# A list scheduler with other durations and a shared-access rule for VectorE and GpSimd

## The chip, the core and the metric

The kernel runs on one core of a Trainium2 chip. The metric is the device time of one execution in microseconds (us), lower is better. TensorE (PE, with its weight loads PEld), VectorE (DVE), ScalarE (ACT), GpSimd (POOL) and the DMA queue of SyncE (SP) each work through a list of instructions of their own, in order, and wait for each other by semaphores.

## What is computed

A small transformer in fp32: 512 tokens, model width 1024, three layers. Layer one has latent attention (12 heads) and cross attention to 256 memory tokens, layer two sliding-window attention (12 query heads, 4 key heads, window 128) and again the cross attention, each with a squared-ReLU MLP of width 4096. The third layer joins a convolution path with a sparse attention of three branches (8 heads) and has a gated convolutional MLP of width 2816.

```
for i in range(2):
    hn = rmsnorm(x, attn_norm_g[i])
    mix, q_cross = (mla_mixer if i == 0 else swa_mixer)(hn, ...)
    cross = memory_cross_attention(q_cross, mem_n, w_mem_kv[i])
    x = x + concat([mix, cross]) @ w_o[i]
    x = x + squared_relu_mlp(rmsnorm(x, mlp_norm_g[i]), w_up[i], w_down[i])
x = rmsnorm(x, final_norm_g)
...
y_b = nsa(q, k_cmp, v_cmp, k_sel, v_sel, k_win, v_win, gates)
mix = gm0 * (y_a @ w_a_out) + gm1 * (y_b @ w_b_out)
x = x + mix @ w_o
x = x + (silu(conv(gate)) * up) @ w_ffn_out
```

## The kernel before

Activations lie transposed, features on the 128 partitions and the 512 tokens along the free axis, so a matrix product is a row of 128x128 weight blocks against 128x512 activations. Every product in the dense layers is made of three matmuls: weights and activations are split into a high part (a cast to fp32r) and a low part (the rest), and high-high, high-low and low-high are added in PSUM. The weights come in chunks of 128x512: a DMA into one of four buffers `raw`, a cast on ScalarE into one of eight buffers `h`, a subtraction on VectorE into one of eight buffers `l` (`fetch_chunk`).

An attention head goes: score matmuls into a PSUM bank `pss`, a fused add-and-minimum on VectorE (the page shows it as CUSTOM_DVE_ANT_0 with a READ_ACCUMULATOR, the order as ISA) that writes the masked scores to SBUF, the exponential on ScalarE with its sum, a reciprocal on VectorE (`rinv`), then `normalize`: four `tensor_scalar` operations on GpSimd, one for each block of 128 queries. TensorE transposes the result into a bank `pst`; ScalarE casts it (high) and VectorE subtracts (low) into tiles `pgr`; value matmuls add into the bank `pso`; `o_out` copies one half on ScalarE and adds on VectorE; `os_set` splits the pair of heads again into high and low. `wo` is the output projection: three jobs are woven, and the k-blocks come in the order 6, 7, 0 to 5, so that the last pair of heads is needed last. Its matmuls and the next heads' projections, in the three banks `psd`, are what TensorE can do while it waits for a softmax.

None of this is issued as written. `Trace` records all 13187 operations with their tiles, `add` gives each a cost by `_op_cost` and finds the operations it depends on, and `schedule` is a greedy list scheduler: it keeps one clock per engine (`engt`), takes the earliest operation that can start, the first recorded one among the ready (a few are recorded as earlier by a bias), and gives out buffers as it goes. A result becomes visible to another engine after `AFTER` of the producer plus `BEFORE` of the consumer. The result is one order for all operations; `emit` issues each in that order, and each engine gets its part as its list. The planned times are not kept: on the chip an engine waits for operands and buffers only.

All recorded instructions carry the one line of the call in `emit` (L426 in the profile), so groups go by tile: `psd`, `pss`, `pst` and `pso` are the banks, `pgf` fp32 pages of 128x512, `pgr` their fp32r kind, `sm` small tiles, `x` the residual, `raw`, `h`, `l` the weights.

## Time and profile before

| | |
|---|---|
| median of 3 runs | 1854.27 us (1851.56 to 1854.47) |
| the profiled execution, its own time | 1850.78 us |
| its span, first to last instruction | 1849.0 us, mean granted clock 0.999 |
| TensorE busy | 1829.8 us, 99% |
| VectorE, ScalarE, GpSimd busy | 1166.8, 856.3, 168.1 us |
| waits of weight loads for the transposes on GpSimd | 9.7 us, 23 times |

The stages by the timeline: first projections to 76 us, latent and cross attention to 198 us, output projection and MLP to 620 us, the second layer's attention to 714 us, its projection and MLP to 1101 us, the third layer's projections and attention to 1320 us, its merging and gates to 1488 us, the last MLP to the end. A matmul's busy time overlaps the next one's, so a busy TensorE may still hold small gaps; those show as waits by releaser, and as idle time in brackets in a timeline.

### The profile page before, as it was taken

What the parts mean: (1) busy time and instruction counts of PE and PEld (TensorE: products, weight loads), DVE (VectorE), ACT (ScalarE), POOL (GpSimd) and SP (SyncE); (2) the same over time, 40 slices, a digit from 0 to 9 for tenths busy, and PEclk for the clock granted to TensorE, in tenths of its full rate; (3) what the DMA queues carried; (4) which work ended last, traced back from release to release, by engine and by line L of the source; (5) the groups of instructions that cost most, each with busy time, mean ns of one, the idle gap of its engine ahead of it and who ended that gap; (6) DMA issues with size and microseconds to landing.
All of it is one profiled execution on the core that took longest, in us unless ns stands there. A gap on an engine that the chain in (4) does not pass through costs nothing.

```text
span 1849.0 us, 24977 instructions
## 1 busy us (share of the span) xinstructions
PE 1829.8 (99%) x8767; PEld 1516.9 (82%) x8767; DVE 1166.8 (63%) x2383; ACT 856.3 (46%) x1700; POOL 168.1 (9%) x228
## 2 busy tenths in 40 slices
PE   8999999999999999999999999999999999999999
PEld 6877888888888888888888887888888888888887
DVE  8998954344446897545434476888655567763752
ACT  7788544242324786443423245476533344442421
POOL 0033100000000241000000000134100011110100
PEclk9999999999999999999999999999999999999999
DMA  6421233333333212333333323212133333333332
GB/s 197 128 58 47 75 97 98 97 97 97 98 97 91 63 52 75 97 97 103 97 97 97 97 67 89 74 47 80 58 97 97 97 97 95 99 93 101 97 97 76
DMA packets 92151, 167.01 MB, mean 90 GB/s; under 512 B 10612, under 2 KB 12408, under 8 KB 92024
## 3 DMA queue, kind: packets, MB, share of 16 engines
q1 hardware_dynamic: 92024, 165.40, 30.1%
q8 instruction: 69, 1.13, 0.2%
q14 instruction: 58, 0.48, 0.1%
HBM read 161.69 MB, written 2.10 MB: 89 GB/s over the span
## 4 chain that ended last, share of the span: by engine, by line
PE 92%; DVE 2%; ACT 2%; issue 1%; POOL 1%; DMA 1%; SPq 1%; POOLq 0%; DVEq 0%; ACTq 0%
PE psd L426 82%; PE pst L426 4%; PE pss L426 4%; PE pso L426 3%; DVE pgf L426 1%; POOL pgf L426 1%; DMA raw<-w 1%; ACT pgf L426 1%; SPq L426 1%; DVE pgr L426 0%; ACT pgr L426 0%; ACT h L426 0%; DVE l L426 0%; DVE sm L426 0%; ACT L426 0%
## 5 line engine op out<-in xcount | busy, mean ns | idle before, releaser
L426 PE MATMUL psd<-pgr,h 128*128 128x512 f32 (+1 forms) x4590 | 1429.8, 390 | 9.0 <-ACT pgr L426 8.5
L426 PEld LDWEIGHTS psd<-pgr,h 128*128 128x128 f32 x4590 | 856.1, 188 | 181.8 <-ACT pgr L426 8.9
L426 PE MATMUL psd<-pgr,l 128*128 128x512 f32 (+1 forms) x2295 | 894.7, 390 | 1.1 <-DVE l L426 1.1
L426 DVE TENSOR_TENSOR l<-raw,h 128x512 fp32r<-128x512 f32 (+2 forms) x601 | 434.2, 726 | 449.2 <-ACT h L426 445.7
L426 ACT CAST h<-raw 128x512 fp32r<-128x512 f32 (+2 forms) x601 | 369.0, 616 | 677.0 <-PE psd L426 605.7
L426 PEld LDWEIGHTS psd<-pgr,l 128*128 128x128 f32 x2295 | 431.0, 188 | 88.5 <-DVE l L426 1.8
L426 POOL TENSOR_SCALAR pgf<-pgf,sm 128x256 f32<-128x256 f32 (+3 forms) x128 | 76.3, 613 | 618.7 <-DVE sm L426 591.9
L426 ACT CAST pgr<-pgf 128x512 fp32r<-128x512 f32 (+4 forms) x184 | 108.2, 590 | 46.3 <-POOL pgf L426 29.9
L426 DVE TENSOR_TENSOR pgr<-pgf,pgr 128x512 fp32r<-128x512 f32 (+4 forms) x184 | 121.5, 662 | 10.7 <-ACT pgr L426 5.6
L426 ACT ACTIVATE pgf<-pgf 128x512 f32<-128x512 f32 (+2 forms) x125 | 74.7, 603 | 108.5 <-DVE pgf L426 106.8
L426 POOL TENSOR_SCALAR pgf<-pgf,sm,gates 128x128 f32<-128x128 f32 (+1 forms) x64 | 49.9, 793 | 549.5 <-PE psd L426 477.8
L426 DVE TENSOR_TENSOR pgf<-psd,pgf 128x512 f32<-128x512 f32 (+2 forms) x94 | 61.3, 654 | 46.5 <-PE psd L426 45.9
L426 PE MATMUL pso<-pgr,pgr 128*128 128x512 f32 (+3 forms) x368 | 89.4, 339 | 0.1
L426 DVE TENSOR_TENSOR pgr<-pst,pgr 128x512 fp32r<-128x512 f32 (+1 forms) x126 | 73.9, 610 | 9.0 <-ACT pgr L426 8.3
L426 POOL TENSOR_TENSOR pgf<-pgf,pgf 128x512 f32<-128x512 f32 x30 | 40.7, 1358 | 422.9 <-DVE pgf L426 412.9
L426 PE MATMUL pst<-cstt,pgf 128*128 128x128 f32 x436 | 76.1, 276 | 2.9 <-POOL pgf L426 2.7
L426 ACT CAST pgr<-pst 128x512 fp32r<-128x512 f32 (+1 forms) x126 | 62.9, 530 | 25.7 <-PE pst L426 23.7
L426 DVE CUSTOM_DVE_ANT_0 pgf<-pss,cmask 128x256 f32<-128x256 f32 (+3 forms) x144 | 65.1, 468 | 9.6 <-PE pss L426 7.9
L426 DVE TENSOR_TENSOR x<-psd,x 128x512 f32<-128x512 f32 x80 | 55.1, 690 | 25.0 <-PE psd L426 24.9
L426 ACT ACTIVATE pgf<-pgf,sm 128x256 f32<-128x256 f32 (+3 forms) x128 | 66.0, 518 | 8.1 <-DVE sm L426 7.4
L426 DVE TENSOR_TENSOR pgf<-pgf,pgf 128x512 f32<-128x512 f32 (+2 forms) x103 | 66.4, 656 | 5.2 <-DMA pgf<-pgf 4.5
L426 PEld LDWEIGHTS pso<-pgr,pgr 128*128 128x128 f32 x368 | 58.8, 189 | 13.0 <-issue 2.5
(120 smaller groups left out, 1075.3 us busy)
## 6 DMA issues: line engine op xcount, KB each, us to landing
raw<-w SPq DMA_DIRECT2D x588, 256.0 KB, 2.6
x<-xT SPq DMA_DIRECT2D x8, 256.0 KB, 5.9
out<-x SPq DMA_DIRECT2D x8, 256.0 KB, 2.0
pgf<-pgf SPq DMA_DIRECT2D x24, 64.0 KB, 2.0
pgf<-aux SPq DMA_DIRECT2D x5, 256.0 KB, 2.7
pgf<-memT SPq DMA_DIRECT2D x4, 256.0 KB, 4.6
raw<-w SPq DMA_DIRECT2D x7, 140.0 KB, 2.1
raw<-w SPq DMA_DIRECT2D x4, 192.0 KB, 2.6
```

The costliest lines, as they stand in the source:

```text
L426: getattr(getattr(nc, names[o.eng]), o.method)(*[r(x) for x in o.args], **{k: r(v) for k, v in o.kw.items()})
```

## The change

The change touches the planner alone. The recorded operations, their dependencies, the priorities, the buffers and the delays `AFTER` and `BEFORE` stay. `_op_cost` gets other durations: a 512-column fp32r matmul counts 226.7 ns where it counted 215.8, a 256-column one 120 in place of 109, a 256 KB load on SP 655 in place of 831, ScalarE 95 ns more for each operand that is one column, 110 in place of 220 for an accumulated sum, GpSimd 25 or 50 ns more. And `schedule` knows a port: an operation of GpSimd other than a memset, and an operation of VectorE of four kinds with all its tiles in SBUF, starts in the plan only when the other engine's last such operation has ended.

```diff
--- before.py
+++ after.py
@@ -303,8 +303,20 @@
 BEFORE = {"PE": 135.0, "DVE": 0.0, "ACT": 0.0, "POOL": 45.0, "SP": 0.0}
 
 
+PORT = ("DVE", "POOL")
+
+
+def _uses_port(o):
+
+    if o.eng == "POOL":
+        return o.method != "memset"
+    if o.eng != "DVE" or any(v.tile.whole for v in o.reads + o.writes):
+        return False
+    return o.method in ("tensor_tensor", "scalar_tensor_tensor", "tensor_scalar", "tensor_copy")
+
+
 class Op:
-    __slots__ = ("i", "eng", "method", "args", "kw", "reads", "writes", "cost", "preds", "succs", "tiles",
+    __slots__ = ("port", "i", "eng", "method", "args", "kw", "reads", "writes", "cost", "preds", "succs", "tiles",
                  "prio", "bias", "npred", "est", "end")
 
 
@@ -319,21 +331,26 @@
     if eng == "PE":
         if method == "transpose":
             return 109.0
-        m, k = _free(args[1]) / 1.2, _free(args[2]) * 0.4167
-        return (max(2 * m, 4 * k) if args[2].dtype == FT else max(m, k)) + 2.5
+        k = _free(args[2])
+        if args[2].dtype == FT:
+            return 2 * max(111.0, (2 * k + 8) / 2.4)
+        return max(105.0, (k + 32) / 2.4)
     if eng == "SP":
-        return 60.0 + n * writes[0].shape[0] * 4 / 340.0
+        return max(600.0, n * writes[0].shape[0] * 4 / 400.0)
+    scalars = [x for x in list(args[2:4]) + [kw.get(k) for k in ("scalar", "bias", "scale")]
+               if isinstance(x, View) and _free(x) == 1]
     if eng == "ACT":
-        return 0.833 * n + (52 if psum else 93) + (220 if accum else 0)
-    scalars = [x for x in list(args[2:4]) + [kw.get("scalar")] if isinstance(x, View) and _free(x) == 1]
+        return 0.833 * n + (52 if psum else 93) + 95 * len(scalars) + (110 if accum else 0)
     if eng == "POOL":
         if method == "memset":
             return 0.833 * n + 60
         if method == "tensor_tensor":
-            return 2.2 * n + 100
-        return 0.833 * n + 160 + 64 * len(scalars)
+            return 2.2 * n + 150
+        return 0.833 * n + 185 + 64 * len(scalars) + (340 if scalars and scalars[0].tile.name.startswith("vecs") else 0)
     n = max([n] + [_free(v) for v in reads if method == "tensor_reduce"])
-    extra = 68 + (60 if scalars or accum else 0)
+    extra = 68 + (60 if scalars else 0) + (75 if accum else 0)
+    if n == 1:
+        return 70.0
     if method in ("tensor_copy", "tensor_scalar", "memset") and not psum:
         return 0.521 * n + extra
     return 1.042 * n + extra
@@ -414,6 +431,7 @@
         out_costs = writes if writes else [v for v in reads]
         o.cost = _op_cost(eng, method, args, kw, reads, out_costs)
         o.eng = eng
+        o.port = _uses_port(o)
         self.ops.append(o)
 
     def emit(self, tc, order):
@@ -457,6 +475,8 @@
         done = np.zeros(n, bool)
         cur = 0
         engt = {e: 0.0 for e in ENGINES.values()}
+        portt = {e: 0.0 for e in PORT}
+        other = {"DVE": "POOL", "POOL": "DVE"}
         ready = {e: [] for e in engt}
         future = {e: [] for e in engt}
         parked = {}
@@ -494,7 +514,8 @@
                     heapq.heappop(q)
                     offer(o)
                     continue
-                return (engt[e] if r else f[0][0]), o.i
+                at = engt[e] if r else f[0][0]
+                return (max(at, portt[other[e]]) if o.port else at), o.i
 
         for o in ops:
             if o.npred == 0:
@@ -515,6 +536,8 @@
             o.est = st
             o.end = st + o.cost
             engt[e] = o.end
+            if o.port:
+                portt[e] = o.end
             order.append(i)
             done[i] = True
             while cur < n and done[cur]:

```

The program places all but the first few rows of every list otherwise. Three places follow; line 444 is the call in `emit` after the change.

VectorE in the sliding-window stage, from the reciprocal of the head whose normalisation begins at 658.27 us in the profile; an `l<-raw,h` is a weight split, `pgr<-pgf,pgr` the low half of a head's output or query, ISA the masked scores from PSUM. Before:

```order
L426 RECIPROCAL sm_22_1145<-sm_19_1088 128x4
L426 ISA pgf_259,sm_21_1134<-pss_165,pgf_321,sm_0_119 128x256
L426 ISA sm_21_1134 128x1
L426 TENSOR_TENSOR pgr_156<-pgf_117,pgr_707 128x512
L426 TENSOR_TENSOR l_262<-raw_88,h_242 128x512
L426 TENSOR_TENSOR sm_0_309<-sm_0_309,sm_4_491 128x4
L426 RECIPROCAL sm_23_1186<-sm_0_309 128x4
```

And now:

```order
L444 RECIPROCAL sm_23_1170<-sm_19_1080 128x4
L444 ISA pgf_288,sm_20_1120<-pss_172,pgf_332,sm_0_123 128x256
L444 ISA sm_20_1120 128x1
L444 TENSOR_TENSOR pgr_925<-pgf_162,pgr_925 64x512
L444 TENSOR_TENSOR pgf_199<-pso_1078,pgf_262 64x512
L444 ISA pgf_137,sm_20_1120<-pss_145,pgf_177,sm_0_123 128x256
L444 ISA sm_20_1120 128x1
L444 ISA pgf_137,sm_20_1120<-pss_172,pgf_177,sm_0_123 128x256
```

Two wide operations with all operands in SBUF stood behind the second mask step; now one of 64 partitions does, then an addition that reads PSUM and two more mask steps.

TensorE at the end of the sliding-window stage: `pso` are the last head's value matmuls, `psd` the output projection. Before (the last two value matmuls, and the projection up to the first matmuls that read the last heads, in the last rows):

```order
L426 MATMUL pso_1084<-pgr_572,pgr_585 128x128
L426 MATMUL pso_1084<-pgr_198,pgr_585 128x128
L426 MATMUL psd_131<-pgr_150,h_208 128x512
L426 MATMUL psd_131<-pgr_482,l_221 128x512
L426 MATMUL psd_137<-pgr_482,h_201 128x512
L426 MATMUL psd_137<-pgr_150,h_201 128x512
L426 MATMUL psd_137<-pgr_482,l_214 128x512
L426 MATMUL psd_133<-pgr_482,h_105 128x512
L426 MATMUL psd_133<-pgr_150,h_105 128x512
L426 MATMUL psd_133<-pgr_482,l_107 128x512
L426 MATMUL psd_131<-pgr_645,h_208 128x512
L426 MATMUL psd_137<-pgr_645,h_201 128x512
```

And now, the first rows again the last value matmuls, and then at once those that read the last heads:

```order
L444 MATMUL pso_1078<-pgr_389,pgr_558 128x256
L444 MATMUL pso_1078<-pgr_564,pgr_277 128x128
L444 MATMUL pso_1078<-pgr_389,pgr_277 128x128
L444 MATMUL psd_135<-pgr_819,h_206 128x512
L444 MATMUL psd_133<-pgr_819,h_192 128x512
L444 MATMUL psd_139<-pgr_819,h_106 128x512
```

Eight matmuls of the projection moved from behind the last value matmul to places ahead of it. At the end of the first attention the same kind of place has 28 such matmuls before and five now.

TensorE in the sliding-window stage near 686 us in the profile, at the first value matmul of a head (`pso`). Before:

```order
L426 MATMUL pso_1084<-pgr_317,pgr_767 128x256
L426 MATMUL psd_133<-pgr_662,h_127 128x512
L426 MATMUL psd_133<-pgr_684,l_139 128x512
L426 MATMUL psd_131<-pgr_899,h_92 128x512
L426 MATMUL psd_131<-pgr_910,h_92 128x512
L426 MATMUL psd_131<-pgr_899,l_96 128x512
L426 MATMUL pst_408<-cstt_135,pgf_162 128x128
L426 MATMUL pso_1084<-pgr_788,pgr_767 128x256
L426 MATMUL pso_1084<-pgr_317,pgr_298 128x256
L426 MATMUL pso_1084<-pgr_788,pgr_298 128x256
```

And now, with the last two of the transposes it depends on ahead of it:

```order
L444 MATMUL pst_409<-cstt_127,pgf_239 128x128
L444 MATMUL pst_312<-cstt_127,pgf_239 128x128
L444 MATMUL pso_1078<-pgr_564,pgr_275 128x256
L444 MATMUL pss_172<-pgr_784,pgr_323 128x256
L444 MATMUL pss_172<-pgr_129,pgr_323 128x256
L444 MATMUL pso_1078<-pgr_848,pgr_275 128x256
L444 MATMUL pso_1078<-pgr_564,pgr_188 128x256
L444 MATMUL pso_1078<-pgr_848,pgr_188 128x256
```

The first value matmul had projection matmuls around it; now it follows the transposes directly, and its low half follows two score matmuls later.

## Rows read from the trace of the kernel before

**Rows 1.** Page, busy time of each engine: us (share of the span) and instructions.

```profile
PE 1829.8 (99%) x8767; PEld 1516.9 (82%) x8767; DVE 1166.8 (63%) x2383; ACT 856.3 (46%) x1700; POOL 168.1 (9%) x228
```

**Rows 2.** The chain that ended last, 242 to 600 us: start us, us, what.

```profile
242.62 344.58 PE psd L426 x1520
```

**Rows 3.** Busy time by stage: stretch, its length, busy us (x) by engine, clock, DMA.

```profile
76.00:198.00 122.00, 120.56 (x666) 94.75 (x665) 111.35 (x308) 104.12 (x262) 39.13 (x64) 1.00 0.20 58
...
620.00:714.00 94.00, 91.55 (x556) 76.76 (x554) 83.41 (x243) 79.30 (x224) 37.15 (x64) 1.00 0.15 45
...
1180.00:1320.00 140.00, 140.00 (x779) 117.51 (x778) 121.79 (x381) 94.69 (x230) 49.92 (x64) 1.00 0.17 52
```

**Rows 4.** Waits over the span: engine and tile <- releaser: us, times, longest.

```profile
PEld pst L426 <- POOL pgf L426: 9.7, 23, 1.0
...
PE psd L426 <- ACT pgr L426: 8.5, 2, 8.3
...
PE pst L426 <- POOL pgf L426: 2.7, 8, 0.6
...
PE psd L426 <- DVE l L426: 1.1, 2, 0.7
```

**Rows 5.** The transposes' tile, 620 to 714 us: who ended TensorE's idle time.

```profile
  POOL pgf L426: 8.1, 19
```

**Rows 6.** Waits from 76 to 198 us.

```profile
PEld pst L426 <- POOL pgf L426: 3.4, 10, 0.9
...
PE pst L426 <- POOL pgf L426: 0.5, 1, 0.5
```

**Rows 7.** Groups by shape on GpSimd, 686.8 to 688.7 us: busy, mean ns.

```profile
L426 POOL TENSOR_SCALAR pgf<-pgf,sm 128x256 f32<-128x256 f32 x3 | 1.4, 478 | 0.0
```

**Rows 8.** Groups by shape on GpSimd, 658.64 to 659.9 us.

```profile
L426 POOL TENSOR_SCALAR pgf<-pgf,sm 128x256 f32<-128x256 f32 x1 | 1.4, 1429 | 0.0
```

**Rows 9.** Timeline of VectorE from 657.8 us: start us, us, instruction.

```profile
658.02 0.45 DVE L426 CUSTOM_DVE_ANT_0 pgf<-pss,pgf,sm 128x256 f32<-128x256 f32 x1
...
658.40 0.78 DVE L426 TENSOR_TENSOR pgr<-pgf,pgr 128x512 fp32r<-128x512 f32 x1
659.11 0.68 DVE L426 TENSOR_TENSOR l<-raw,h 128x512 fp32r<-128x512 f32 x1
```

**Rows 10.** Timeline of TensorE from 658.5 us, [idle before <-releaser].

```profile
660.10 0.44 PE L426 MATMUL pst<-cstt,pgf 128*128 128x128 f32 x2 [0.56 <-POOL pgf L426]
...
661.44 0.44 PE L426 MATMUL pst<-cstt,pgf 128*128 128x128 f32 x2 [0.21 <-POOL pgf L426]
```

**Rows 11.** Timeline of GpSimd, 1250.62 to 1253.2 us.

```profile
1250.56 2.90 POOL L426 TENSOR_SCALAR pgf<-pgf,sm,gates 128x512 f32<-128x512 f32 x1
```

**Rows 12.** Groups by shape on GpSimd, 1285.1 to 1285.8 us.

```profile
L426 POOL TENSOR_SCALAR pgf<-pgf,sm,gates 128x512 f32<-128x512 f32 x1 | 0.8, 766 | 0.0
```

**Rows 13.** Timeline of VectorE, 1250.5 to 1253.5 us.

```profile
1250.87 1.27 DVE L426 TENSOR_TENSOR l<-raw,h 128x512 fp32r<-128x512 f32 x2
...
1252.16 0.65 DVE L426 TENSOR_TENSOR l<-raw,h 128x512 fp32r<-128x512 f32 x1
```

**Rows 14.** The chain that ended last, 710 to 716 us: start us, us, what.

```profile
711.14 0.77 PE pso L426 x7
...
711.98 0.59 ACT pgf L426
...
712.59 0.70 DVE pgf L426
...
713.31 0.63 ACT pgr L426
...
713.99 2.14 PE psd L426 x8
```

**Rows 15.** The transposes' tile, 620 to 714 us: duration ns min/median/max of its readers.

```profile
L426 ACT CAST pgr<-pst x32: 483/586/595, 626.8 to 709.7; 128x512 fp32r<-128x512 f32 x20, 128x384 fp32r<-128x384 f32 x12
L426 DVE TENSOR_TENSOR pgr<-pst,pgr x32: 527/672/692, 627.9 to 710.5; 128x512 fp32r<-128x512 f32 x20, 128x384 fp32r<-128x384 f32 x12
```


## The prediction

> **What bounds the kernel now.** I read the page's busy shares first, then the busy time by stage, the chain of waits, the waits by releaser, and last the timeline around single waits. TensorE is busy 99% of the span [rows 1], and in the long matrix stages it has no gap at all: 1520 matmuls of 512 columns take 344.58 us, so 0.227 us each [rows 2]. No plan can change that, because the change neither adds nor removes an instruction. The granted clock is full, 1.00 in each stage of [rows 3]. What a new order can win or lose lies in the attention stages, where TensorE's list mixes matmuls that wait for a softmax with matmuls that wait for nothing ("cover" from here on). In the sliding-window stage (620 to 714 us) VectorE is busy 83.41 of 94 us and TensorE 91.55; in the first attention (76 to 198 us) VectorE 111.35 of 122 [rows 3]. There the two engines are nearly level, so a plan that starves either shows at once. In the block from 1180 to 1320 us TensorE is busy throughout [rows 3].
>
> The waits say who was late. Over the whole span the largest releaser of TensorE after the start-up (8.5 us) is GpSimd: 9.7 us before weight loads of the transposes and 2.7 us before the transposes themselves [rows 4]. Of these 12.4 us, 8.1 us in 19 waits lie in the sliding-window stage [rows 5] and 3.4 + 0.5 us in the first attention [rows 6]. These transposes read what GpSimd has just normalised, and GpSimd was late because it shares SBUF access with VectorE: a normalisation of 128x256 takes 0.478 us undisturbed [rows 7] and 1.429 us where VectorE runs two wide operations beside it [rows 8, 9]; TensorE then waits 0.56 and 0.21 us [rows 10].
>
> **What the change does to the lists.** The recorded operations and their priorities are the same; only the planner's clock differs. Three things follow, which I price one by one.
>
> *First, collisions.* The plan now lets a GpSimd operation and an SBUF-only VectorE operation exclude each other. The chip gets no wait for that, only the two lists. I therefore counted, in VectorE's own list, the SBUF-only operations of 128 elements or more that stand behind a group's reciprocal within the length of the group's four normalisations: 65 in 48 groups before, 59 now. By stage: the sliding window 16 before and 10 now, first attention with its cross attention and the second cross attention 27 and 28, the last attention 22 and 21. So the plan clears a third of the collisions in one stage and next to none elsewhere. The first excerpt of the order shows one that improves: two wide operations behind the reciprocal become one. With the 8.1 us of [rows 5] in proportion, 8.1 x 6/16 = **-3.0 us**. From below it could be the whole 12.4 us of [rows 4]; from above nothing, or a loss, if the transposes were moved forward as much as GpSimd gets faster. I take the proportion, since the waits are of this one stage.
>
> How kind the plan is to GpSimd can be read from one more place: a normalisation of 128x512 takes 2.900 us [rows 11], where 0.766 us is its undisturbed time [rows 12]; in that stretch VectorE ran three weight splits [rows 13]. So GpSimd can lose to several VectorE operations in a row, while the plan makes it lose to one, and I leave the -3.0 as it is. The Trainium skill, page "SBUF — State Buffer", section "Who interferes with whom", says that whoever issues first holds the shared pair for its whole instruction and the other blocks. Taken one instruction at a time, that rule would have made this normalisation late by a single operation of 0.69 us, 1.46 us in all; the trace does not agree. By that rule the plan would be right about every collision, and the sum would be that of the first rival below.
>
> *Second, the ends of two stages.* The planner now believes the attention chain to be slower, so its greedy choice spends the cover earlier. In the second excerpt, eight cover matmuls stand between the last value matmul of the sliding window and the first output projection that needs it; now there is none. That chain is in the trace: value matmuls to 711.91, a ScalarE copy of 0.59, a VectorE add of 0.70, a ScalarE cast of 0.63, and TensorE goes on at 713.99 [rows 14], 2.08 us later, almost all of it covered. Eight matmuls of 0.227 us are 1.8 us of cover lost: **+1.8 us**. At the end of the first attention, the same chain had 28 cover matmuls behind its last value matmul and has five now; 5 x 0.227 = 1.1 us against 2.08 gives **+1.0 us**. What is queued behind those waiting matmuls is the rest of the output projection, so nothing else can fill in. Both could be less if the chain itself ends earlier; not below nothing.
>
> *Third, a hole inside the sliding window.* In the third excerpt a value matmul stood behind five cover matmuls and its tail behind more; now it stands right behind the transposes it depends on. Between them lie a ScalarE cast and, for the low half, a VectorE subtraction. A cast of this kind takes 0.586 us and a subtraction 0.672 us [rows 15]; with some 0.2 us from the transposes to the cast's start the operand comes 0.8 us after the transposes, with 0.1 us of cover now: +0.7, and the low half 0.67 us later against 0.24 us of scores in between: +0.4. Together **+1.1 us**.
>
> The rest I cost at nothing. The list of the SP queue differs in a handful of rows, at the start and around two row swaps near 1140 us; weights are held eight chunks deep, which is the cover for that, and if it failed, a late chunk would cost what TensorE's longest wait for a weight split costs today, 1.1 us in two waits [rows 4]. GpSimd's additions in the last two stages stay slow, but TensorE has no gap there [rows 2]. Places that become tighter or looser everywhere else I bound by the heads: TensorE's work between a head's last score matmul and its first transpose, less VectorE's work between the same two points, each added up from the two lists with the trace's durations, falls from 15.4 to 10.5 us over the twelve heads of the sliding window, so +5 at most; in the first attention it rises for seven of twelve heads, by 5.7 us in all, so -6 at best. I take 0, near the middle.
>
> **Sum.** -3.0 + 1.8 + 1.0 + 1.1 = +0.9 us against the profiled execution's own 1850.8 us (its span 1849.0 and 1.8 around it). That execution lies 3.5 us under the median of the three runs, 1854.3, so I forecast 1854.3 + 0.9 = **1855.2 us**: no difference that can be told, since runs of this kernel tell apart about 0.2%, which is 3.7 us.
>
> **Rivals.**
> 1. *The collisions go as planned, and the kernel gets faster.* VectorE's wide operations depend on casts that the plan also moved, so they may really arrive after GpSimd. For it: in the planner's joint order only a few wide operations still start inside a group. Against it: VectorE's own list hardly thins, and nothing holds VectorE back. Then 8.1 + 3.9 us of waits go [rows 5, 6] and the stage ends cost 2.8: 1854.3 - 9.2 = 1845.1 us. It decides if GpSimd's waits fall under 4 us in all. It is also where the rule that the Trainium skill gives on its page "SBUF — State Buffer" would lead.
> 2. *TensorE runs out of cover in the sliding window, and the kernel gets slower.* VectorE is busy 89% there [rows 3], and the weight splits that make cover possible queue behind it. Place: 640 to 715 us; price: the 5 us of lost room above with the 1.8, 1.0 and 1.1, without the gain: +8.9, so 1863.2 us. It decides when the lost room costs over 3 us. For it: the second and third excerpts. Against it: fewer collisions in just this stage.
> 3. *The change does not do on the chip what it says*, because lists without waits leave the timing as it was, the collisions and the cover both: 1854.3 us.
>
> **How the numbers follow.** My forecast has 0.30, the third rival 0.18, the first 0.26 and the second 0.26. The likeliest two agree within 0.2%, so "same" has 0.48, faster 0.26, slower 0.26. Half of each outer rival's mass lies nearer than its full price, so leaving out a tenth at either end gives 1846 to 1862 us; that takes in the bounds of the third term and most of the first.
>
> **What would show it.** Right: GpSimd's waits before the transposes near 9 us in place of 12.4, the fall all in 620 to 714 us; a new wait of about 2 us of the output projection for ScalarE's cast at the end of that stage and of about 1 us near 200 us; the long run of 1520 matmuls unchanged. Wrong: normalisations at their undisturbed times throughout (then the first rival), or TensorE's busy time between 620 and 714 us stretched by 5 us or more with waits for VectorE (then the second). A changed start, a new stretch at half clock, or a longer chain near 1130 us would be a cause I did not see.

## The result: slower by half a per cent

| | before | after |
|---|---|---|
| median | 1854.37 us (1851.56 to 1854.59, 4 runs) | 1864.01 us (1862.09 to 1866.28, 4 runs) |
| ratio | | 1.0053, 95% interval 1.0041 to 1.0065 |
| profiled execution: own time, span | 1850.78, 1849.0 us | 1862.09, 1860.3 us |

The forecast was 1855.2 us with a range to 1862; the time lies above it. The page's line of busy times after the change (columns as in [rows 1]), and three rows of the chain of waits (start us, us, what):

```profile
PE 1835.9 (99%) x8767; PEld 1518.8 (82%) x8767; DVE 1166.0 (63%) x2383; ACT 855.5 (46%) x1700; POOL 158.3 (9%) x228
```

```profile
248.76 344.80 PE psd L444 x1521
...
763.39 344.80 PE psd L444 x1521
...
1504.66 352.07 PE psd L444 x1553
```

The same two later runs of matmuls before the change:

```profile
752.13 344.58 PE psd L426 x1520
1493.57 351.83 PE psd L426 x1552
```

GpSimd works 10 us less: its collisions did become fewer. The first long run of matmuls, at 242.62 us before [rows 2], starts some 6 us later; the second starts 11.3 us later (763.39 against 752.13), the last one 11.1 us later. So the loss arose in the first attention (6.4 us by the start of one and the same matmul) and in the sliding window (5.1 us); the third layer lost nothing (-0.2), and the long runs themselves kept their 0.227 us per matmul.

Two rows of the waits over the span (engine and tile <- releaser: us, times, longest), against [rows 4]:

```profile
PE psd L444 <- ACT pgr L444: 11.5, 3, 8.4
PEld pst L444 <- POOL pgf L444: 6.4, 19, 0.6
```

GpSimd as a releaser of the weight loads fell from 9.7 to 6.4 us. The output projection's wait for ScalarE's cast rose from 8.5 to 11.5 us, which is the start-up's 8.4 and two new waits. They and a hole stand in TensorE's timeline (idle before and releaser in brackets):

```profile
210.48 1.36 PE L444 MATMUL psd<-pgr,h 128*128 128x512 f32 x4 [1.05 <-ACT pgr L444]
...
690.08 0.39 PE L444 MATMUL pso<-pgr,pgr 128*128 128x256 f32 x1 [0.57 <-ACT pgr L444]
...
692.33 0.55 PE L444 MATMUL pso<-pgr,pgr 128*128 128x256 f32 x3 [0.79 <-DVE pgr L444]
...
724.02 1.23 PE L444 MATMUL psd<-pgr,h 128*128 128x512 f32 x4 [2.09 <-ACT pgr L444]
```

These are the places that the three excerpts of the order pointed at: the ends of the two stages and the value matmuls right behind their transposes. Behind the last wait comes something that was not foreseen, in the windows (columns as in [rows 3]):

```profile
724.00:726.00 2.00, 1.98 (x7) 1.55 (x8) 1.17 (x2) 0.64 (x2) 0.00 (x0) 0.84 0.06 16
726.00:728.00 2.00, 2.00 (x6) 1.52 (x6) 1.85 (x4) 2.00 (x4) 0.00 (x0) 0.50 0.00 0
728.00:730.00 2.00, 2.00 (x9) 1.60 (x8) 2.00 (x4) 2.00 (x5) 0.00 (x0) 0.81 0.46 131
```

The granted clock falls to 0.50, the lower of its two levels (1.2 of 2.4 GHz); 0.32 + 1.00 + 0.38 us of work are lost there, 1.7 in all.

For the rest of the text a stage's **lag** is the start of the same matmul in the following long run, less its start in the trace of before, less the lag that the stage began with. Stage one ends at the first long run, stage two at the second, stage three at the end. Inside a stage the lag is taken where TensorE has done the same amount of work, each matmul counted by the median spacing of its kind (bank and shape) in the trace of before. For the changed kernel it is 0.6 us at 40 us, 4.4 at 110, 4.6 at 200, 6.4 at 210; 6.4 at 620, 3.6 at 680, 6.4 at 690, 7.6 at 710 and 11.5 at 720 us. The middle of the sliding window gained 2.8 us, and its last 40 us gave back 7.9. All lags lean to the long side, those of the start and of stage three above all, because the profiled execution of before is a fast one: 1850.78 us, where the medians of its later sets of runs are 1852.38 to 1853.31.

### The profile page after: what moved, and what is told of

It reads as the page before. It is cut to its first block, busy times and chain, and to the rows that moved or that the text cites. A ratio compares the mean times of both kernels' runs of the same rounds, so it can differ in the third digit from the quotient of the medians.

```text
span 1860.3 us, 24961 instructions
## 1 busy us (share of the span) xinstructions
PE 1835.9 (99%) x8767; PEld 1518.8 (82%) x8767; DVE 1166.0 (63%) x2383; ACT 855.5 (46%) x1700; POOL 158.3 (9%) x228
## 3 DMA queue, kind: packets, MB, share of 16 engines
q8 instruction: 68, 1.11, 0.2%
## 4 chain that ended last, share of the span: by engine, by line
PE 90%; DVE 4%; ACT 3%; issue 2%; DMA 1%; POOL 0%; SPq 0%; ACTq 0%; DVEq 0%; POOLq 0%
PE psd L444 81%; PE pss L444 3%; PE pst L444 3%; PE pso L444 3%; DVE pgf L444 2%; ACT pgf L444 1%; ACT pgr L444 1%; DVE pgr L444 1%; DVE l L444 1%; DMA raw<-w 0%; DVE sm L444 0%; POOL pgf L444 0%; ACT h L444 0%; SPq L444 0%; DMA x<-xT 0%
## 5 line engine op out<-in xcount | busy, mean ns | idle before, releaser
L444 PE MATMUL psd<-pgr,h 128*128 128x512 f32 (+1 forms) x4590 | 1430.8, 391 | 12.1 <-ACT pgr L444 11.5
L444 POOL TENSOR_SCALAR pgf<-pgf,sm 128x256 f32<-128x256 f32 (+3 forms) x128 | 70.5, 569 | 633.8 <-DVE sm L444 579.0
L444 PEld LDWEIGHTS pst<-cstt,pgf 128*128 128x128 f32 x436 | 53.3, 140 | 19.8 <-POOL pgf L444 6.4
```

Source lines behind the costliest of these rows:

```text
L444: getattr(getattr(nc, names[o.eng]), o.method)(*[r(x) for x in o.args], **{k: r(v) for k, v in o.kw.items()})
```

## The experiments

All kernels compute the whole reference. Lags are in us from one profile each; ratios are to the kernel before, with 95% intervals.

| kernel | median us | ratio (interval) | lag: stages one, two, three |
|---|---|---|---|
| the change | 1864.01 | 1.0053 (1.0041, 1.0065) | 6.4, 5.1, -0.2 |
| e1 durations only | 1858.26 | 1.0020 (1.0011, 1.0029) | 5.8, 1.6, 0.9 |
| e2 rule only | 1870.52 | 1.0090 (1.0074, 1.0105) | 9.2, 3.9, 5.2 |
| e3 TensorE's durations | 1863.48 | 1.0058 (1.0044, 1.0072) | 3.5, 2.8, 6.6 |
| e5 change in stage one | 1858.03 | 1.0026 (1.0017, 1.0035) | 5.6, 0.0, 4.0 |
| e6 change in stage two | 1858.26 | 1.0024 (1.0015, 1.0034) | 1.5, 3.4, 0.8 |
| e8 the other durations | 1857.45 | 1.0025 (1.0013, 1.0037) | 4.0, 0.8, 3.9 |
| e9 stage two without the last heads | 1856.74 | 1.0018 (1.0009, 1.0028) | 0.0, 2.3, 1.2 |
| e10 VectorE's durations | 1858.55 | 1.0031 (1.0019, 1.0043) | 3.2, 3.9, 1.2 |
| e11 VectorE's delay 125 | 1855.49 | 1.0011 (1.0002, 1.0021) | 3.9, -0.4, 2.9 |
| e12 VectorE's delay 131 | 1856.31 | 1.0020 (1.0010, 1.0029) | 0.6, 1.4, 3.8 |
| e13 matmuls 1 ns longer | 1857.40 | 1.0023 (1.0013, 1.0032) | 1.6, 1.8, 2.7 |
| e14 the change, delay 125 | 1862.64 | 1.0051 (1.0033, 1.0069) | 5.4, 4.9, 1.6 |
| e15 stage two, cover pinned | 1858.50 | 1.0021 (1.0012, 1.0030) | 1.3, 6.6, 3.6 |
| e17 stage two, early scores | 1856.57 | 1.0016 (1.0007, 1.0025) | 1.7, 2.4, 2.4 |
| e18 stage two, earlier scores | 1858.77 | 1.0024 (1.0015, 1.0033) | 0.2, 2.5, 1.0 |
| e19 earlier scores alone | 1852.29 | 0.9994 (0.9985, 1.0003) | 0.5, -1.2, 0.7 |
| e21 the same again | 1850.94 | 0.9990 (0.9981, 0.9999) | 0.2, -1.2, 0.9 |
| e20 earlier scores, GpSimd later | 1849.76 | 0.9979 (0.9970, 0.9988) | 0.6, -3.7, 0.5 |

How much of a lag is chance is read from stages whose list of TensorE is that of before: stage one lags by 0.0 to 1.7 us in nine profiles (e6, e9, e12, e15, e17 to e21; two matmuls have other places in e12), stage three by 0.5 to 4.0 in e5, e6, e9, e15 and e17 to e21. A stage-three lag up to 4 us says nothing.

In stage one the chance lies at the start: the nine profiles lag by 0.1 to 1.7 us at 40 us already, and from 40 to 200 us none of them moves by more than 0.2. Counted from 40 to 200 us, the losses are 4.0 us in the changed kernel, 3.9 in e5, 3.7 in e1, 3.3 in e14, 2.4 in e8, 2.3 in e10, 2.2 in e11, 2.1 in e2, 1.7 in e3 and 0.5 in e13. The changed kernel, e5 and e14 have one list of TensorE up to 110 us, and by then have lost 3.8, 4.0 and 3.5 us of it. Each lag is of one execution; the profile of e15 is the slowest of its ten, that of e18 the fastest of its eleven.

### Rule or durations, first or second stage

**e1**: the rule off. **e2**: the rule on, `_op_cost` as before. The diff of e1 against the change:

```diff
-                return (max(at, portt[other[e]]) if o.port else at), o.i
+                return at, o.i
```

> The changed kernel with its new durations, without the rule that GpSimd and VectorE exclude each other. The theory of the rule (it makes the plan believe the attention chain longer, so the cover of TensorE is spent before the ends of the stages) expects the loss to be gone: the list keeps 21 cover matmuls behind the last value matmul of the first attention (28 before, 5 with the whole change) and 4 at the end of the sliding window (8 and 0); so no wait near 210 us, about 1 us near 720 us, and 1853 to 1857 us. The theory of the durations (227 in place of 216 ns per matmul took away a cushion that covered what the plan does not know) expects the whole loss here: 1862 to 1866 us. The theory of chance (a greedy plan with any other numbers gives another order, worth several us either way, without one cause) expects anything from 1846 to 1868 us, and gains and losses in stages that neither rule nor durations tell apart.

> The kernel before with the exclusion rule alone, at the old durations. The theory of the rule expects the loss here: no cover matmul is left at the end of either stage, so waits of about 2 us each near 210 and 720 us, and 1860 to 1867 us. The theory of the durations expects 1852 to 1857 us. The theory of chance expects anything from 1846 to 1868 us.

Measured: 1858.26 and 1870.52 us; the first lies between the ranges of rule and durations, in that of chance alone. Each part alone is slower, and the rule alone is slower than the whole change. Its price stands at the ends, as the cover in the list said: at the first attention's end the lag jumps from 2.7 to 9.2 us, with a wait for a chain of VectorE and ScalarE in the chain of waits (first fence) and the clock's fall in the windows (second):

```profile
209.59 0.69 DVE pgf L439
...
210.36 0.63 ACT pgr L439
...
211.03 11.06 PE psd L439 x35
```

```profile
208.00:210.00 2.00, 0.46 (x5) 0.32 (x3) 1.97 (x7) 0.58 (x1) 0.00 (x0) 1.00 0.00 0
210.00:212.00 2.00, 0.97 (x2) 0.83 (x3) 1.97 (x6) 0.62 (x1) 0.00 (x0) 0.57 0.00 0
212.00:214.00 2.00, 2.00 (x6) 1.56 (x5) 1.28 (x5) 0.62 (x2) 0.00 (x0) 0.50 0.00 0
```

The time of e2 is above the ranges of all three theories: in its profile a stretch near half clock follows each end's wait, which costs 3.4 us from 210 to 217 us and 1.7 us near 727 us, and its third stage, with another list, lost 5.2 us. In e1 the wait at the second end was 1.11 us, as expected, and none for the cast stood at the first; yet stage one lost 5.8 us, 4.6 of them by 110 us. So the theory of the rule holds for the ends and fails for the beginning.

The rule also has a gain, and of the two parts only the rule: from 620 to 680 us the lag falls by 2.8 us in the changed kernel, by 3.5 in e2 and by 0.0 in e1. The Trainium skill, page "SBUF — State Buffer", section "Who interferes with whom", says that VectorE and GpSimd share one pair of ports and that the one that holds it blocks the other. The trace agrees as far as it goes: with the rule, GpSimd's 64 normalisations from 620 to 722 us took 33.9 us in all where they took 38.3, and its 8.1 us of waits in this stage [rows 5] fell to 2.8 + 0.5 us. What the plan pays for it elsewhere is another matter.

**e5** and **e6** apply the change to some of the recorded operations only:

```diff
+        new = o.i < 3000
-        o.cost = _op_cost(eng, method, args, kw, reads, out_costs)
+        o.cost = (_op_cost if new else _old_cost)(eng, method, args, kw, reads, out_costs)
-        o.port = _uses_port(o)
+        o.port = new and _uses_port(o)
```

(in e6 `new = 3000 <= o.i < 6600`; `_old_cost` is `_op_cost` of before).

> The whole change, for the operations up to the middle of the first MLP alone; later operations keep the old durations and no rule. TensorE's list then differs from that of before in the first attention alone. If the loss sits where the changed kernel's chain shows it, the first long run of 1520 matmuls starts about 5 to 6 us later than before (242.6), the later stages take as long as before, and the time is 1858 to 1861 us. If the loss comes from elsewhere (the granted clock, the weights' transfers, an effect of one stage on the next), the time is within 2 us of 1854.4 or not the sum of the two parts.

> The whole change for the operations from the middle of the first MLP to the middle of the second alone. TensorE's and VectorE's lists are those of the changed kernel in the sliding-window attention and those of before elsewhere. If the loss sits where the chain shows it, the first long run starts at 242.6 as before, the second one 5 us later than before (752.1), and the time is 1858 to 1861 us; there is no cover at the stage's end, so the wait of 2.3 us near 724 us is there, and if the stretch at half clock behind it comes from that wait, it is there too. If the parts do not add, within 2 us of 1854.4.

Measured: 1858.03 and 1858.26 us, ratios 1.0026 and 1.0024; together 1.0050 against the 1.0053 of the whole. So each stage loses without the other's help. But e5 is not quite the first half of the change: from about 150 us on, its list of TensorE is another than the changed kernel's, no wait stands at its first attention's end (lag 5.6 us at 200 and at 210 us), and all of its 5.6 us were lost ahead of it. That the parts add up is in part luck. In e6 the lists of the second stage are those of the changed kernel. The wait at the end was there, with 2.08 us, but the clock stayed at 1.00 behind it:

```profile
718.80:720.80 2.00, 2.00 (x9) 1.53 (x9) 1.17 (x2) 0.74 (x2) 0.00 (x0) 1.00 0.09 26
720.80:722.80 2.00, 2.00 (x10) 1.45 (x9) 2.00 (x5) 2.00 (x4) 0.00 (x0) 1.00 0.00 0
```

### Which duration

**e3**, **e8** and **e10** are the kernel before with some of the new durations: TensorE's alone; all but TensorE's; VectorE's alone, which are these:

```diff
-    extra = 68 + (60 if scalars or accum else 0)
+    extra = 68 + (60 if scalars else 0) + (75 if accum else 0)
+    if n == 1:
+        return 70.0
```

> The kernel before with TensorE's new durations alone (227 in place of 216 ns for a 512-column matmul, 120 in place of 109 for a 256-column one). With all new durations and no rule the first attention lost 5.8 us, nearly all of it before 110 us. The theory of the cushion (matmuls believed 5% shorter than they are put some work behind each chain that the plan did not ask for; the truth takes it away) expects that loss here: the first long run 4 to 6 us later than 242.6, 1857 to 1860 us. The theory of the small operations (ScalarE's, VectorE's, GpSimd's or SyncE's new durations are wrong where the first projections and the cross attention hang on them) expects the first long run within 1.5 us of 242.6 and 1852 to 1855 us. The theory of chance expects some loss or gain of several us in each of both kernels of this pair, and no sum.

> The kernel before with the new durations of ScalarE, VectorE, GpSimd and SyncE, TensorE's as before, no rule. The theory of the small operations expects the loss of the first attention here, the first long run 4 to 6 us later than 242.6; the theory of the cushion expects it within 1.5 us. For the ends of the stages the list tells: 17 cover matmuls behind the last value matmul of the first attention, so no wait near 205 us; none at the end of the sliding window, so a wait of some 2 us near 715 us, without any rule of exclusion. So 1855 to 1857 us by the cushion, 1859 to 1863 us by the small operations.

> The kernel before with VectorE's new durations alone (one-element operations 70 ns, 75 in place of 60 for an accumulated sum). No rule, TensorE as before; still the list has no cover matmul at the end of the sliding window, and 14 behind the last value matmul of the first attention. If the price of a stage's end follows the cover in TensorE's list, whoever moved it, there is a wait of about 2 us near 714 us and none near 205 us. If it follows the rule of exclusion (GpSimd's or VectorE's lists), there is none at either. Time by the cover: 1855 to 1857 us; else 1852 to 1855 us.

Measured: stage one lost 3.5, 4.0 and 3.2 us in the three. Neither the theory of the cushion nor that of the small operations is right by itself: counted from 40 to 200 us, TensorE's durations cost 1.7 us and the others 2.4, together about the 3.7 of e1, and VectorE's alone cost 2.3. The times are 1863.48, 1857.45 and 1858.55 us; e8's lies between the ranges of the two theories, e10's above its own. The time of e3 lies above its range because of a stage three that lost 6.6 us, of which the clock's stretch near 1180 us is a part; no more was found out on that. The second question has a clear answer: e8 and e10 have no rule, their lists have no cover at the end of the sliding window, and both have the wait:

```profile
717.42 2.07 PE L430 MATMUL psd<-pgr,h 128*128 128x512 f32 x4 [2.08 <-ACT pgr L430]
```

```profile
719.63 2.07 PE L428 MATMUL psd<-pgr,h 128*128 128x512 f32 x4 [2.08 <-ACT pgr L428]
```

The first is of e8, the second of e10. The price of this stage's end follows TensorE's list, whoever moved it.

### Is any other order slower

**e11** and **e12**: `"DVE": 125.0` and `"DVE": 131.0` in `AFTER` of the kernel before. **e13**: each matmul 1 ns more. **e14**: the changed kernel with 125.

```diff
-AFTER = {"PE": 197.0, "DVE": 128.0, "ACT": 132.0, "POOL": 75.0, "SP": 2000.0}
+AFTER = {"PE": 197.0, "DVE": 125.0, "ACT": 132.0, "POOL": 75.0, "SP": 2000.0}
```

> A change that says nothing new of the chip: the delay behind VectorE's results in the plan is 125 ns in place of 128. TensorE's list of the first attention changes as much as by the real change (551 of 1059 places; 636 there), that of the sliding window hardly (36 of 797). The cover behind the last value matmul of the first attention is 19 matmuls, enough. So far every new order lost 3 to 9 us in the first attention, whatever part of the change made it. The theory that the order of before is a good draw, kept because it ran well, and that a greedy plan's other orders are ordinary, expects the first long run 2 to 6 us later than 242.6 here too, the second stage as before within 1 us, and 1855 to 1860 us. The theory that durations and rule have each their own fault expects it within 1.5 us, and 1852 to 1855 us.

> The same with 131 ns. Here TensorE's list is that of before in the first attention (2 places differ) and another one in the sliding window (378 of 797 places, 7 cover matmuls at its end in place of 8) and in the third layer (486 of 1186). The theory of the good draw expects the first long run at 242.6, the second 1 to 4 us later than 752.1, the third layer some us longer, and 1854 to 1860 us. The theory of faults expects 1852 to 1855 us.

> Each matmul is believed 1 ns longer than in the kernel before (0.5%, where the change has 5%). TensorE's list differs in 420 of 1059 places of the first attention, 407 of 797 of the sliding window (13 cover matmuls at its end, more than the 8 of before), 513 of 1186 of the third layer's attention. The theory of the good draw expects losses in the first attention and in the third layer as in the others, 1856 to 1864 us; the theory of faults, and that of the cushion in particular, expects a tenth of the loss of TensorE's durations, 1852 to 1855 us.

> The changed kernel with the delay behind VectorE's results 125 ns in place of 128. The sliding window's list is that of the changed kernel (7 places differ); the cover behind the last value matmul of the first attention is 27 matmuls in place of 5. If the price of that end follows the cover, the wait near 210 us is gone; the sliding window loses some 5 us as in the changed kernel. The theory of the good draw expects the first attention to stay 3 to 6 us late for its first 110 us, and the total 1860 to 1866 us; the theory of faults expects the first attention's early loss to be the same 4 us as in the changed kernel, within 0.5 us, since its cause is the same.

Measured: the three small shifts, which say nothing new of the chip, cost 0.11 to 0.23%, 2 to 4 us, all three in the range of the theory of the good draw and above that of faults; with e11 it is stage one (3.9 us, outside the spread of 0 to 1.7), with e12 and e13 it is spread thin (1.4 and 1.8 us in stage two). A new list does not cost in every stage, though: e13 has another one in 420 of 1059 places of the first attention, and its stage one lags by 1.6 us, no more than chance. So three neutral shifts out of three lose 2 to 4 us, and the order of before is better than these neighbours; a part of that size of the change's 10 us needs no fault in the durations or the rule. Why the order of before is better, the runs don't say. e14 doesn't tell the two theories apart: from 40 to 110 us it lost 3.5 us, the changed kernel 3.8, and its 1862.64 us lie in the range of the good draw. In e14 the first attention's end had its cover back in the list, and TensorE ran through it:

```profile
210.16 0.61 PE L444 MATMUL psd<-pgr,h 128*128 128x512 f32 x2
210.62 0.39 PE L444 MATMUL psd<-pgr,l 128*128 128x512 f32 x1
210.84 0.61 PE L444 MATMUL psd<-pgr,h 128*128 128x512 f32 x2
```

The lag from 200 to 210 us is 0.1 us in place of 1.8. With e5, this is the second list with another order of the last heads and no wait: that term is shown. The second stage lost 4.9 us as in the changed kernel, with nearly the same list.

### The end of the sliding window: cover or chain

**e9** ends the change at the eighth head (`new = 3000 <= o.i < 5100`). **e15** is e6 with nine matmuls of the projection pinned behind the last value matmul:

```diff
+PIN = {5392: range(5469, 5478)}
...
+        for p, r in PIN.items():
+            for j in r:
+                ops[j].preds.add(p)
```

> The whole change for the operations from the middle of the first MLP up to the eighth head of the sliding window alone; the last heads, and everything else, keep the old durations and no rule. The eight cover matmuls at the end of the sliding window are back in the list. If the change is good for GpSimd in the middle of this stage (2.8 us were gained there up to 680 us, in the whole change and in the second-stage kernel) and bad only where it spends the cover ahead of the end, the second long run starts 1 to 3 us earlier than 752.1 and the time is 1850.5 to 1853 us, faster than both kernels. If the gain in the middle is work taken from the end (TensorE did early what it then lacks), the gain is given back behind 680 us whatever the list says, and the time is 1853 to 1858 us.

> The change in the second stage alone, and nine matmuls of the output projection, which do not need the last heads, are pinned in the plan behind the last value matmul, so that 2.04 us of cover stand at the end (0 without the pin, 1.8 before). Everything else of the two lists is nearly the same (36 of 797 places of TensorE's list differ). If cover at the end is what lacks, the wait of 2.3 us of the projection is gone and the second long run starts 0 to 1.5 us later than 752.1; 1853 to 1855.5 us. If the stage is bound by the chain behind the last scores (the last score matmul started 12.4 us ahead of the first matmul that needs the last pair of heads, in the second-stage kernel as in before 12.9, though TensorE had 8.7 us of work in between in place of 12.2), the wait only moves ahead, to the last head's value matmuls, the second long run is 3 to 5 us late, and the time is 1856.5 to 1859 us.

Measured, e9: 1856.74 us, no gain, and in the range of the second theory, by which the gain in the middle is work taken from the end. It was 3.2 us ahead at 680 us and 2.3 behind at 720: the end's wait was 0.2 us, but without the rule the last heads waited for GpSimd again, in a stretch that had less to cover it:

```profile
PEld pst L472 <- POOL pgf L472: 4.9, 8, 1.0
...
PE pst L472 <- POOL pgf L472: 3.0, 6, 0.8
```

e15: 1858.50 us beside 1858.26 of e6, in the range of the chain. Its lag of 6.6 us in the table is beyond that theory's 3 to 5, but up to 5.1 of it was lost at half clock, from 687 to 694 us and near 719 us, so only the place of its waits is read here. The projection's wait is gone, and a wait stands one step earlier, at the last head's value matmuls, as the theory of the chain had it:

```profile
716.71 0.39 PE L473 MATMUL pso<-pgr,pgr 128*128 128x256 f32 x1 [1.18 <-ACT pgr L473]
717.50 1.72 PE L473 MATMUL pso<-pgr,pgr 128*128 128x256 f32 x7 [0.40 <-DVE pgr L473]
```

The chain itself is seen in the rows of the score tile, which name the start of the last score matmul (before, changed, e2, e6, e20; each from a window of its own, so only the last start is to be read):

```profile
L426 PE MATMUL pss<-pgr,pgr x100: 218/282/373, 630.3 to 701.0; 128*128 128x256 f32 x76, 128*128 128x128 f32 x24
```

```profile
L444 PE MATMUL pss<-pgr,pgr x116: 221/282/387, 629.8 to 711.4; 128*128 128x256 f32 x92, 128*128 128x128 f32 x24
```

```profile
L439 PE MATMUL pss<-pgr,pgr x120: 220/282/378, 631.3 to 712.9; 128*128 128x256 f32 x96, 128*128 128x128 f32 x24
```

```profile
L472 PE MATMUL pss<-pgr,pgr x104: 220/281/384, 632.2 to 706.4; 128*128 128x256 f32 x80, 128*128 128x128 f32 x24
```

```profile
L426 PE MATMUL pss<-pgr,pgr x100: 218/282/384, 630.9 to 697.3; 128*128 128x256 f32 x76, 128*128 128x128 f32 x24
```

The first projection matmul that needs the last heads starts at 713.99 before [rows 14], 724.02 in the changed kernel, and in e2 and e6, by their chains, at

```profile
725.75 9.32 PE psd L439 x33
```

```profile
718.80 16.37 PE psd L472 x70
```

That is 13.0, 12.6, 12.9 and 12.4 us behind the last score. The windows between the two moments show what TensorE had to do in them (before, changed, e2, e6):

```profile
701.00:713.99 12.99, 12.81 (x76) 10.48 (x75) 8.94 (x22) 8.73 (x24) 5.39 (x8) 1.00 0.23 62
```

```profile
711.40:724.02 12.62, 9.67 (x55) 7.50 (x54) 8.40 (x20) 7.46 (x20) 4.41 (x8) 1.00 0.36 106
```

```profile
712.90:725.75 12.85, 8.02 (x45) 5.38 (x43) 7.84 (x20) 6.51 (x18) 4.86 (x8) 1.00 0.25 79
```

```profile
706.40:718.80 12.40, 9.70 (x57) 7.57 (x55) 8.20 (x20) 7.25 (x19) 4.39 (x8) 1.00 0.38 106
```

The same 12.4 to 13 us with 76, 55, 45 and 57 matmuls in them: softmax, normalisation, casts and value matmuls of the last head are a chain of that length, and work that the plan did before the last score can no more cover it. The changed plan leaves 21 fewer behind it. That is where a part of the gain of the middle went; the hole near 690 us took the other.

If so, the last scores must come earlier. **e17** and **e18** record the last heads as earlier operations, on top of e6; **e19** and its repetition **e21** do what e18 does, on the kernel before:

```diff
-        o.bias = self.bias
+        o.bias = self.bias - (60 * (5103 <= len(self.ops) < 5138) + 60 * (5182 <= len(self.ops) < 5228)
+                              + 120 * (5228 <= len(self.ops) < 5263) + 120 * (5307 <= len(self.ops) < 5353))
```

> The change in the second stage alone, with the last query projection and the scores and softmax of the last two heads recorded as 60 operations earlier, so that the plan takes them before other ready work. In TensorE's list 13.9 us of work (by the floor of each matmul in the trace of before) then stand between the last score and the first matmul that needs the last heads; 8.7 without it, 12.2 before. If the chain behind the last scores binds, no wait above 0.6 us is left at the end, and the second long run starts between 2 us earlier and 0.5 us later than 752.1: 1851 to 1854.5 us. If it is cover as such that lacks, or if early scores only push other heads back, 2 to 5 us later: 1855 to 1859 us.

> The same, and the pair of heads ahead of it 60 operations earlier too: 15.5 us of TensorE work behind the last score. By the chain: no wait at the end, the second long run at most 1 us away from that of the kernel with 13.9 us, since work beyond the chain's 12.5 us covers nothing; 1850.5 to 1854.5 us. By the other theory 1855 to 1860 us.

> The kernel before with the same earlier recording of the last two pairs of heads, without the change: 15.9 us of TensorE work behind the last score, and as many wide VectorE operations behind the reciprocals as before (18, with the change 10). If the change is good for GpSimd in the middle of the stage, this kernel keeps GpSimd's waits (8 us in this stage) and its second long run is 1 to 3 us later than that of the kernel with change and earlier recording. If the change brings nothing, the two agree within 1 us. 1851 to 1856 us.

> The kernel with the earlier recording alone a second time. If it is faster than before, by the 0.9 us that the first set showed, 1851.5 to 1852.8 us beside 1853.2; if the first set was chance, a ratio of 0.9995 to 1.001. Both theories of the change expect it to be faster than the changed kernel by 10 us or more.

Measured: the projection waited at most 0.2 us at the end in e17 and e19, and 0.6 in e18 (of weight loads). But e17 and e18 gained little, 1856.57 and 1858.77 us, outside the ranges that the chain gave and inside those of the other theory, by which early scores only push other heads back. The wait at the end is explained by the chain; the loss of the stage is not, it moved. In e18 one wait of 3.00 us stands at the transposes of 690 us, for the low half of another head, and the clock falls behind it:

```profile
690.01 0.41 PE L472 MATMUL pst<-cstt,pgf 128*128 128x128 f32 x2 [3.00 <-DVE pgr L472]
```

Without the change the same recording lost nothing anywhere: 1852.29 and 1850.94 us, and stage two 1.2 us ahead in both profiles. Against both expectations e19 was ahead of e18, by 3.4 us at the second long run. The medians are 6.5 us apart, the profiles 3.7, all of it in stage two: that is what the change costs when the end is taken care of. e21 came out faster than either of its ranges, so the early recording alone gains 1 to 2 us by the medians, clear of noise in the second set alone. e19 still had GpSimd's waits (5.0 + 1.9 us in the stage).

### Distance in place of the rule

**e20** is e19, with GpSimd's results in stage two believed 300 ns later, so that the plan puts more of TensorE's work between a normalisation and its transposes, and keeps VectorE's list free of a rule:

```diff
-            vis = o.end + AFTER[e]
+            vis = o.end + AFTER[e] + (300 if e == "POOL" and 3000 <= i < 6600 else 0.0)
```

> The kernel with the earlier recording alone, and in the second stage GpSimd's results believed 300 ns later, in place of a rule of exclusion. In TensorE's list 13.8 us of work then stand behind the last score and 14 cover matmuls at the end (15.9 us and 14 without it). If GpSimd's waits can be bought off by distance without a price at the end, the 6.9 us of waits before the transposes fall under 4 us and the second long run starts 2 to 4 us earlier than 752.1; 1848.5 to 1851 us. If what is gained there comes back as other waits, as in all kernels with the rule, the second long run is within 1.5 us of the kernel with the earlier recording alone; 1851 to 1855 us.

Measured: 1849.76 us, 0.9979 (0.9970 to 0.9988) of the time of before: faster than both kernels, as the first theory had it, and 1.2 us faster than e21, which ran in the same set (the means differ by 2.0 us, with a 95% interval of 0.8 to 3.2). The distance was not tried without the earlier recording. The waits for GpSimd from 620 to 714 us, first e20, then e19:

```profile
PEld pst L426 <- POOL pgf L426: 1.6, 4, 0.6
...
PE pst L426 <- POOL pgf L426: 0.2, 1, 0.2
```

```profile
PEld pst L426 <- POOL pgf L426: 5.0, 9, 1.0
PE pst L426 <- POOL pgf L426: 1.9, 6, 0.6
```

They fell from 6.9 to 1.8 us, the second long run starts at 749.07 us (752.13 before), and TensorE is busy without a gap from the last score on:

```profile
697.30:711.30 14.00, 14.00 (x87) 12.21 (x86) 10.40 (x20) 9.40 (x22) 3.72 (x8) 1.00 0.20 59
```

## Why the prediction was wrong, point by point

- **Collisions, -3.0 us: right place, the size by luck.** The middle of the sliding window gained 2.8 us, and all kernels with the rule there did (e2, e6, e9, e14, e15, e17, e18: 2.4 to 3.5 us by 680 us); without it the lag of e1, e3, e8 and e10 moved by +0.2 to -1.7, and only e20 gained as much, by distance. (e8 gained 2.7 by 710 us.) GpSimd's waits fell further than the 9 us foreseen, to 6.4 + 0.9 us over the span; from 620 to 680 us they fell from 5.0 + 1.9 us to

```profile
PEld pst L444 <- POOL pgf L444: 0.3, 1, 0.3
```

  So the working took 6/16 of the waits where nearly all went, and counted a microsecond of a weight load's wait as one of TensorE's, where 6.6 us of waits were worth 2.8 us; the two errors cancel. The gain also did not last to the stage's end, in any kernel with the rule.
- **Stage ends, +1.8 and +1.0 us: right mechanism, too small.** The waits were 2.09 us at the sliding window's end and 1.05 us at the first attention's. The lag over them was 3.9 and 1.8 us: at the former, 1.7 us at half clock came on top. e14, e8 and e10 show that the wait follows the list; e15 shows that cover behind the last value matmul alone only moves it.
- **The hole, +1.1 us: right place, mis-sized.** The two waits for cast and subtraction were 0.57 and 0.79 us, the lag from 680 to 690 us 2.8, and 1.2 more to 710 us.
- **"The rest I cost at nothing": this failed.** Between 40 and 200 us the first attention lost 4.0 us in places that no term had. No single one is large. Waits from 20 to 110 us, after:

```profile
PEld pss L444 <- DVE sm L444: 1.9, 3, 1.0
PEld pst L444 <- DVE sm L444: 1.4, 3, 0.6
...
PE pss L444 <- DVE sm L444: 1.1, 2, 0.8
PEld psd L444 <- DVE pgf L444: 0.8, 1, 0.8
```

  All four are waits for VectorE; before, the first and third came to 1.2 and 0.2 us in the same stretch and the others did not occur. The step took 0 between +5 and -6 because the distances added up over twelve heads had risen there. It left out the first projections and the cross attention, and that is where it failed: 3.8 of the 4.0 us were lost between 40 and 110 us, while the twelve heads, whose scores start at 107.8 us, lost some 0.2. Why these places wait longer in the new order is not shown. Of the other orders, e3, e8, e10 and e11 lost 1.7 to 2.4 us between 40 and 200 us, e13 0.5, where the unchanged list moves by 0.2 at most; the forecast was centred as if a new order were as likely better as worse, and none here was better in that stage. (That TensorE has no gap in the last two stages the prediction reads from [rows 2], which show another stretch; the third stage lost nothing all the same.)
- **The account.** Start-up 0.6, first attention 4.0 and its end 1.8, the window's middle -2.8, hole 2.8, next 20 us 1.2, end 3.9, third layer -0.2: 11.3 us, the difference of the two spans. Against the forecast's +0.9 that is 10.4 us more: 5.6 from what was taken at nothing, 2.9 from the ends, 1.7 from the hole, 0.2 from the collisions. The 0.6 of the start-up is within chance.
- **The rivals.** The second one (cover runs out in the sliding window, 1863.2 us) came nearest, but only half for its reason: that stage lost 5.1 us, more than the 3 from which it was to decide, while of the other 6.4 it had priced 1.0. Its mechanism, weight splits that queue behind VectorE's other work, is not what the waits name: TensorE waited 0.2 us for a split there (620 to 714 us). At the end it is the chain behind the last score. The first rival's test (GpSimd's waits under 4 us) failed with 7.3; the third, no effect, is refuted.

What stays open: why the first projections and the cross attention lose in the changed kernel's order, why stage one of the kernel before is better than its neighbours, why the rule's kernels lose near 690 us what they gained even where the end is taken care of (e17, e18), and what made the clock fall behind some waits and not behind others.

## What to carry over

A more truthful cost in a greedy planner need not give a better plan: here, with the rule, it left 21 fewer matmuls behind the last head's scores, and the chain behind them stayed as long as it was. Before spending independent work in the middle of a stage, measure the chain from its last input to its first dependent matmul (here 12.4 to 13 us) and see in the list that this much work stands beside it. To relieve a slow producer, try distance behind it in the plan (e20, 1.2 us faster than e21 without it) before a rule that holds other engines back (e18, 6.5 us slower than e19 without the change), and compare any planner change with small neutral shifts of its constants, which cost 2 to 4 us here.

## What was not expected of the hardware

Behind a wait of 2.08 or 2.09 us at the same place of the program the granted clock fell to 0.50 in the changed kernel, e2, e8, e10 and e14, but not in e6, whose lists are those of the changed kernel in this stage; the difference between the second-stage lags of 5.1 and 4.9 us (changed, e14) and 3.4 us (e6) is about the 1.7 us that such a stretch loses. In e15 it fell near 687 us, at waits of 0.57 and 0.78 us, where the changed kernel and e6, with the same waits, stayed at 1.00. And every profile, that of before too (1168 to 1172 us), has a stretch at the lower level somewhere between 1128 and 1188 us; what stood in front of it was not compared.
